# Moving the second layer's memory values ahead of the first layer's output projection

## The chip, the cores and the metric

The kernel runs on one core of a Trainium2 chip. The metric is the device time of one execution in microseconds. Three runs of the kernel before took 1002.79, 1003.25 and 1001.37 us, a median of 1002.79 us.

The engines are named as in the profile: PE is TensorE's matrix multiplication, PEld its loading of weights, DVE is VectorE, ACT is ScalarE, POOL is GpSimd, and SP is the engine whose queue issues all transfers. L120 is line 120 of the kernel.

## The reference

An encoder trunk of two layers works on 256 tokens of width 1024, in float32. Each layer computes:

```
h = x @ w_in                     # latents, differential q/k/v, memory queries, gates
o_mla, o_diff, o_mem = three attention branches
merged = sum of sigmoid(gate_i) * (o_i @ w_branch_i)
x = LayerNorm(alpha * x + merged @ w_out)
x = LayerNorm(alpha * x + relu(x @ w1)^2 @ w2)
```

The third branch is an attention into 256 memory tokens. Its keys and values are `mem @ mem_w_kv[l]`, split into two halves of 512 columns each. They depend on the memory and on the layer's weights alone, not on `x`, so those of the second layer can be computed at any time.

## The kernel before, in words

**Precision.** Every float32 operand is split into a high part, rounded by ACT, and a low part, the rest, computed by DVE. A product is made of three matmuls, high by high, high by low and low by high (`mm3`, L126 to L129). A weight block of 128 x 1024 values (512 KB) is loaded by SP into one of six `raw` buffers, and `wload` (L111) casts it on ACT (L120) and subtracts on DVE (L121) into one of eight `whl` buffers. A second ring, `whlx`, serves the held-back half of `w_out` and of the last `w2` blocks. `evac` (L151) brings a PSUM tile into SBUF in the same two parts, ACT first (L153), then DVE (L154).

**PSUM.** There are four `acc` tiles and four `sm` tiles, one bank each.

**Order.** The program is written as one long trace. A planner, which runs a model of the engines, then sets each engine's queue: what stands earlier in the trace goes first where it is ready by the model, and what stands later is pulled forward into free time. Each engine then works through its queue in order on the chip. In the attention part of a layer a list written by hand (`ORDER`) sets the order of the trace; its last steps in the first layer are those of branch E, whose results are transposed on PE (L714) and evacuated (L156 on ACT, L157 on DVE) into the operands of the output projection.

**Around the change.** After the last step of `ORDER` the first layer goes on in this order of the trace:

- the parameters of the first normalisation and the residual input `xn` are loaded;
- `load_memT` (L294) loads the transposed memory again and splits it;
- the output projection `wout` takes 96 matmuls in four accumulators: first blocks 0 to 3 for both halves of the tokens and both halves of the columns, then blocks 4 to 7 for the first 128 tokens, then for the others. In the profile these accumulators have the name `load_memT.acc`;
- the first 128 tokens are normalised and `fill_xT` (L195) transposes them in two groups of four on PE (L200) and evacuates each group (L153, L154) into a half of `xT`;
- `mem_keys` (L305) makes the second layer's memory keys, with four weight blocks;
- the other 128 tokens are normalised and filled into `xT`;
- `mem_values` (L320) makes the second layer's memory values: four weight blocks, two `sm` accumulators, 48 matmuls of 512 columns, and two evacuations;
- `mlp1(0)` (L942) begins. Its matmuls (`mm_wide`, L131) take the weights as the stationary operand and stream both parts of `xT` for all 256 tokens at once:

```
def both(k):
    PE.matmul(ps, lhsT=ws[k // 4][0][:, k % 4, sl], rhs=r2(k), start=k == 0, stop=k == KD - 1)
```

  so that the first of them needs the high and the low part of the first half of `xT` for the second 128 tokens too.

In the second layer there is no memory work. There the second fill of `xT` is followed at once by `MlpTokens.project(1)` (L554), which takes the `xT` of 128 tokens as the stationary operand by `mm3`: two matmuls with the high part, then one with the low part.

Of the kernel before, what the change touches and what calls it, by code (L numbers as in the profile page):

```python
# [21 lines left out]
DEPTH = 2  # L22
# [44 lines left out]
def encoder_trunk(ctx: ExitStack, tc: tile.TileContext, x, w_in, b_gate,  # L67
# [16 lines left out]
    def nm(s):  # L84
        uid[0] += 1
        return f"{stage[0]}.{s}_{uid[0]}"

    def acc_tile():
        return pp.tile([P, 512], F32, tag="acc", name=nm("acc"))
# [4 lines left out]
    def slot():  # L94
        return act.tile([P, 2, 512], F32R, tag="att", bufs=BUFS["att"], name=nm("att"))
# [15 lines left out]
    def wload(src, a, b, ring="whl", raw=None):  # L111
        if raw is None:
            raw = wraw(src, a, b)
        hl = wp.tile([P, 2, 1024], F32R, tag=ring, bufs=BUFS[ring], name=nm("whl"))
        hi, lo = (hl[:, s, :a * b].rearrange("p (a b) -> p a b", a=a) for s in range(2))
        split(hi, lo, raw)
        return hi, lo

    def split(hi, lo, src):
        S.copy(out=hi, in_=src)  # L120
        V.tensor_tensor(lo, src, f32v(hi), ALU.subtract)  # L121

    def wsrc(w2d, k0, nk, n0, nn):
        return w2d[k0 * P:(k0 + nk) * P, n0:n0 + nn].rearrange("(k p) n -> p k n", p=P)

    def mm3(ps, lh, ll, rh, rl, start, stop):  # L126
        PE.matmul(ps, lhsT=lh, rhs=rh, start=start, stop=False)  # L127
        PE.matmul(ps, lhsT=lh, rhs=rl, start=False, stop=False)  # L128
        PE.matmul(ps, lhsT=ll, rhs=rh, start=False, stop=stop)  # L129
# [21 lines left out]
    def evac(dst_h, dst_l, ps, scale=None):  # L151
        if scale is None:
            S.copy(out=dst_h, in_=ps)  # L153
            V.tensor_tensor(dst_l, ps, f32v(dst_h), ALU.subtract)  # L154
        else:
            S.activation(dst_h, ps, AF.Copy, scale=scale)  # L156
            V.scalar_tensor_tensor(dst_l, ps, scale, f32v(dst_h), ALU.mult, ALU.subtract)  # L157
# [37 lines left out]
    def fill_xT(xT, nat, t):  # L195
        for h in range(2):
            ps = sm_tile()
            for i in range(4):
                k = h * 4 + i
                PE.transpose(ps[:, i * P:(i + 1) * P], nat[:, k * P:(k + 1) * P], ident)  # L200
            pv = ps.rearrange("p (k q) -> p k q", k=4)
            ts = slice(t * P, (t + 1) * P)
            evac(xT[h][:, 0, :, ts], xT[h][:, 1, :, ts], pv)

    def xk(xT, k, t=None):
        v = xT[k // 4]
        ts = slice(0, T) if t is None else slice(t * P, (t + 1) * P)
        return v[:, 0, k % 4, ts], v[:, 1, k % 4, ts]
# [85 lines left out]
    def load_memT():  # L294
        stage[0] = "load_memT"
        mT = []
        for h in range(2):
            raw = wp.tile([P, 4, T], F32, tag="raw", bufs=BUFS["raw"], name=nm("memr"))
            nc.sync.dma_start(out=raw, in_=wsrc(mem_t, 4 * h, 4, 0, T))
            m = act.tile([P, 2, 4, T], F32R, tag="mT", bufs=2, name=nm("mT"))  # L300
            split(m[:, 0], m[:, 1], raw)
            mT.append(m)
        return mT
# [16 lines left out]
    def mem_values(l, mT, ptile):  # L320
        stage[0] = "mem_vals"
        pss = [ptile() for _ in range(2)]
        for c in range(4):
            wh, wl = wload(wsrc(w_mkv[l], 2 * c, 2, 512, 512), 2, 512)
            for i in range(2):
                k = 2 * c + i
                for t in range(2):
                    mh, ml = xk(mT, k, t)
                    mm3(pss[t], mh, ml, wh[:, i], wl[:, i], k == 0, k == KD - 1)
        Vt = []  # L330
        for t in range(2):
            v = slot()
            evac(v[:, 0, :], v[:, 1, :], pss[t])
            Vt.append(v)
        return Vt
# [269 lines left out]
    for l in range(DEPTH):  # L605
# [4 lines left out]
        if l == 0:  # L610
            K, Vt = [], []
# [292 lines left out]

        if l + 1 < DEPTH:
            memT = load_memT()
        pss = [acc_tile() for _ in range(4)]
        stage[0] = "wout"
        wo = {}
# [15 lines left out]
        for t in range(2):  # L925
# [9 lines left out]
                halfway = [m.project(0) for m in early]  # L935
            layernorm(xns[t], pss[2 * t:2 * t + 2], gb)
            fill_xT(xT, xns[t], t)
        if l + 1 < DEPTH:
            Vt = mem_values(l + 1, memT, sm_tile)


        def mlp1(j):  # L942
            stage[0] = "mlp1"
# [117 lines left out]
```

## Time and profile before

| | us |
|---|---|
| median of three runs | 1002.79 |
| the profiled execution's own time | 1001.16 |
| its span, first to last instruction | 999.4 |
| PE busy in the span | 985.4 (99%) |
| PEld busy | 851.3 (85%) |
| DVE busy | 753.4 (75%) |
| ACT busy | 588.8 (59%) |
| mean granted TensorE clock | 0.997 of full speed |

Matmuls overlap in the profile: one of 512 columns is listed with 0.39 us, and in a dense stretch the next starts 0.23 us after it. So the distance from one start to the next tells what a matmul costs, and the idle time listed for PE begins only where the listed end of the last one has passed. Transfers moved 181 MB, 181 GB/s over the span.

### The profile page before, as it was taken

Reading aid. Unit: us, or ns where it says so; the run is one execution under the profiler, and the core shown is the slowest. Engines: PE = TensorE matmul, PEld = TensorE weight load, DVE = VectorE, ACT = ScalarE, POOL = GpSimd, SP = SyncE. Lnnn points to the kernel's source line nnn. Section 1 sums busy time; section 2 is a strip of 40 time slices with the busy share of each in tenths; the row PEclk is TensorE's granted clock in tenths of the full one; section 3 lists DMA queues with packets and bytes.
Section 4 is the critical chain, followed back from the end, with each engine's and each line's share of the span. In section 5 each row is a group of like instructions: output and inputs, shape, how many; then the busy total and the mean of one; then the engine's idle time right before and its main releaser. Section 6 shows DMA issues by size and latency. Waiting matters only on the chain.

```text
span 999.4 us, 14511 instructions
## 1 busy us (share of the span) xinstructions
PE 985.4 (99%) x5315; PEld 851.3 (85%) x5315; DVE 753.4 (75%) x1164; ACT 588.8 (59%) x1060; POOL 45.6 (5%) x86
## 2 busy tenths in 40 slices
PE   9999999999999999999999999999999999999996
PEld 7888989888888888888889989898888878888885
DVE  6897889777897676656775988798688876666664
ACT  5975777766662554444624877778665525454540
POOL 0200001100000000000001110000000000000000
PEclk9999999999999999999999999999999999999998
DMA  9965455555794466665844755456457725766631
GB/s 302 319 209 146 121 148 169 171 156 159 243 308 123 151 192 196 195 192 175 292 130 154 228 151 148 129 158 186 130 157 261 232 76 177 228 186 191 188 127 43
DMA packets 103200, 181.06 MB, mean 181 GB/s; under 512 B 5965, under 2 KB 59481, under 8 KB 103129
## 3 DMA queue, kind: packets, MB, share of 16 engines
q1 hardware_dynamic: 103128, 180.14, 58.3%
q8 instruction: 42, 0.69, 0.3%
q14 instruction: 30, 0.24, 0.1%
HBM read 178.02 MB, written 2.10 MB: 180 GB/s over the span
## 4 chain that ended last, share of the span: by engine, by line
PE 94%; DVE 2%; ACT 2%; DMA 1%; issue 1%; POOL 0%; SPq 0%; DVEq 0%; ACTq 0%
PE mlp1.sm L135 11%; PE mlp1.sm L138 6%; PE mlp2.acc L127 6%; PE mlp2.acc L129 6%; PE mlp2.acc L128 6%; PE diff_proj.acc L127 5%; PE diff_proj.acc L128 5%; PE diff_proj.acc L129 5%; PE gate.acc L127 2%; PE gate.acc L128 2%; PE gate.acc L129 2%; PE branch.acc L127 2%; PE branch.acc L129 2%; PE branch.acc L128 2%; PE diff_att.sm L519 2%; PE mla_att.acc L128 1%
## 5 line engine op out<-in xcount | busy, mean ns | idle before, releaser
L121 DVE TENSOR_TENSOR mlp1.whl<-mlp1.raw,mlp1.whl 128x1024 fp32r<-128x1024 f32 x124 | 150.9, 1224 | 88.1 <-ACT mlp1.whl L120 85.4
L120 ACT CAST mlp1.whl<-mlp1.raw 128x1024 fp32r<-128x1024 f32 x124 | 129.9, 1052 | 88.7 <-PE mlp2.acc L129 41.7
L135 PE MATMUL mlp1.sm<-wout.xT,mlp1.whl 128*128 128x512 f32 x480 | 122.5, 392 | 0.0
L135 PEld LDWEIGHTS mlp1.sm<-wout.xT,mlp1.whl 128*128 128x128 f32 x480 | 86.3, 189 | 15.2
L127 PE MATMUL mlp2.acc<-mlp1.whl,mlp1.att 128*128 128x512 f32 x240 | 93.4, 389 | 0.0
L129 PE MATMUL mlp2.acc<-mlp1.whl,mlp1.att 128*128 128x512 f32 x240 | 93.4, 389 | 0.0
L128 PE MATMUL mlp2.acc<-mlp1.whl,mlp1.att 128*128 128x512 f32 x240 | 93.4, 389 | 0.0
L121 DVE TENSOR_TENSOR gate.whl<-gate.raw,gate.whl 128x1024 fp32r<-128x1024 f32 x48 | 58.4, 1219 | 18.0 <-ACT gate.whl L120 17.5
L138 PEld LDWEIGHTS mlp1.sm<-wout.xT,mlp1.whl 128*128 128x128 f32 x480 | 65.5, 190 | 4.7
L121 DVE TENSOR_TENSOR diff_proj.whl<-diff_proj.raw,diff_proj.whl 128x1024 fp32r<-128x1024 f32 x44 | 53.7, 1221 | 19.2 <-ACT diff_proj.whl L120 18.6
L138 PE MATMUL mlp1.sm<-wout.xT,mlp1.whl 128*128 128x256 f32 x480 | 66.9, 282 | 0.0
L120 ACT CAST gate.whl<-gate.raw 128x1024 fp32r<-128x1024 f32 x48 | 50.4, 1052 | 17.9 <-PE diff_proj.acc L129 5.8
L120 ACT CAST diff_proj.whl<-diff_proj.raw 128x1024 fp32r<-128x1024 f32 x44 | 46.5, 1056 | 21.2 <-PE diff_proj.acc L129 11.4
L537 ACT COPY mlp1.sum<-mlp1.sm 128x256 f32<-128x256 f32 x60 | 22.3, 372 | 54.8 <-PE mlp1.sm L135 54.8
L128 PEld LDWEIGHTS mlp2.acc<-mlp1.whl,mlp1.att 128*128 128x128 f32 x240 | 45.1, 188 | 9.4
L129 PEld LDWEIGHTS mlp2.acc<-mlp1.whl,mlp1.att 128*128 128x128 f32 x240 | 45.1, 188 | 9.4
L127 PEld LDWEIGHTS mlp2.acc<-mlp1.whl,mlp1.att 128*128 128x128 f32 x240 | 45.1, 188 | 9.4
L121 DVE TENSOR_TENSOR branch.whl<-branch.raw,branch.whl 128x1024 fp32r<-128x1024 f32 x32 | 39.1, 1221 | 14.7 <-ACT branch.whl L120 14.3
L120 ACT CAST branch.whl<-branch.raw 128x1024 fp32r<-128x1024 f32 x32 | 33.6, 1050 | 27.0 <-PE gate.acc L129 12.2
L127 PE MATMUL diff_proj.acc<-diff_proj.whl,mlp1.xT 128*128 128x512 f32 (+1 forms) x128 | 43.4, 340 | 0.2 <-ACT mlp1.xT L153 0.2
L128 PE MATMUL diff_proj.acc<-diff_proj.whl,mlp1.xT 128*128 128x512 f32 (+1 forms) x128 | 43.1, 338 | 0.0
L129 PE MATMUL diff_proj.acc<-diff_proj.whl,mlp1.xT 128*128 128x256 f32 (+1 forms) x128 | 42.9, 338 | 0.0
(472 smaller groups left out, 2533.9 us busy)
## 6 DMA issues: line engine op xcount, KB each, us to landing
mlp1.raw<-in_mlp_w_dram SPq DMA_DIRECT2D x124, 512.0 KB, 4.4
gate.raw<-in_w_in_dram SPq DMA_DIRECT2D x48, 512.0 KB, 3.7
branch.raw<-in_w_branch_dram SPq DMA_DIRECT2D x32, 512.0 KB, 3.8
diff_proj.raw<-in_w_dqk_dram SPq DMA_DIRECT2D x28, 512.0 KB, 4.2
diff_proj.raw<-in_w_in_dram SPq DMA_DIRECT2D x16, 512.0 KB, 3.8
wout.raw<-in_w_out_dram SPq DMA_DIRECT2D x16, 512.0 KB, 4.6
mq.raw<-in_w_in_dram SPq DMA_DIRECT2D x8, 512.0 KB, 4.7
mem_keys.raw<-in_mem_w_kv_dram SPq DMA_DIRECT2D x8, 512.0 KB, 5.6
```

What stands on the lines that cost most here:

```text
L120: S.copy(out=hi, in_=src)
L121: V.tensor_tensor(lo, src, f32v(hi), ALU.subtract)
L127: PE.matmul(ps, lhsT=lh, rhs=rh, start=start, stop=False)
L128: PE.matmul(ps, lhsT=lh, rhs=rl, start=False, stop=False)
L129: PE.matmul(ps, lhsT=ll, rhs=rh, start=False, stop=stop)
L135: PE.matmul(ps, lhsT=ws[k // 4][0][:, k % 4, sl], rhs=r2(k), start=k == 0, stop=k == KD - 1)
L138: PE.matmul(ps[:, 0, :], lhsT=ws[k // 4][1][:, k % 4, sl], rhs=r2(k)[:, 0, :], start=False, stop=False)
L519: PE.matmul(po[:, t * T:(t + 1) * T], lhsT=pT[:, hl, kt * T + t * P:kt * T + (t + 1) * P], rhs=vh[:, :, kt * T + j * P:kt * T + (j + 1) * ...
L537: S.copy(out=d, in_=ps[:, 1, :])
```

## The change

The call of `mem_values` for the second layer moves in the trace from behind the loop over the two token halves to the place right behind `load_memT`, ahead of the output projection. Nothing of what is computed changes, nor any size, buffer count or pool; `mem_values` still takes its two accumulators from the `sm` tiles. Its weight loads move ahead of those of `w_out` and of `mem_keys` in the trace.

```
         if l + 1 < DEPTH:
             memT = load_memT()
+            Vt = mem_values(l + 1, memT, sm_tile)
         pss = [acc_tile() for _ in range(4)]
         stage[0] = "wout"
...
             layernorm(xns[t], pss[2 * t:2 * t + 2], gb)
             fill_xT(xT, xns[t], t)
-        if l + 1 < DEPTH:
-            Vt = mem_values(l + 1, memT, sm_tile)
-
```

## Rows read from the trace of the kernel before

**Rows 1.** Page: busy us by engine; chain that ended last, share by engine.
```profile
PE 985.4 (99%) x5315; PEld 851.3 (85%) x5315; DVE 753.4 (75%) x1164; ACT 588.8 (59%) x1060; POOL 45.6 (5%) x86
...
PE 94%; DVE 2%; ACT 2%; DMA 1%; issue 1%; POOL 0%; SPq 0%; DVEq 0%; ACTq 0%
```

**Rows 2.** Waits of PE, whole span: waiter, releaser, total us, times, longest.
```profile
PE diff_proj.acc L274 <- ACT diff_proj.nat L763: 1.7, 1, 1.7
...
PE mlp1t.sm L571 <- DVE mlp1t.fr L544: 0.6, 1, 0.6
PE load_memT.acc L127 <- ACT branch.att L156: 0.5, 1, 0.5
...
PE mlp1t.sm L127 <- ACT wout.xT L153: 0.2, 1, 0.2
```

**Rows 3.** Timeline of PE, 296 to 306 us: start, us, instruction, [idle before, releaser].
```profile
296.26 1.04 PE L714 MATMUL branch.sm<-consts,branch.merged 128*128 128x128 f32 x8
297.84 0.50 PE L127 MATMUL load_memT.acc<-wout.whl,branch.att 128*128 128x512 f32 x1 [0.54 <-ACT branch.att L156]
...
299.77 0.60 PE L714 MATMUL branch.sm<-consts,branch.merged 128*128 128x128 f32 x4
300.30 0.50 PE L129 MATMUL load_memT.acc<-wout.whl,branch.att 128*128 128x512 f32 x1
...
304.97 0.60 PE L714 MATMUL branch.sm<-consts,branch.merged 128*128 128x128 f32 x4
305.32 0.48 PE L129 MATMUL load_memT.acc<-wout.whl,branch.att 128*128 128x512 f32 x1
```

**Rows 4.** Timeline of PE, 332 to 346 us.
```profile
332.91 1.04 PE L200 MATMUL layernorm.sm<-consts,branch.xn 128*128 128x128 f32 x8
333.70 0.47 PE L127 MATMUL mem_vals.sm<-mem_vals.whl,load_memT.mT 128*128 128x512 f32 x1
...
344.71 1.07 PE L135 MATMUL mlp1.sm<-wout.xT,mlp1.whl 128*128 128x512 f32 x4
```

**Rows 5.** Timeline of ACT and DVE, 333 to 337 us.
```profile
333.38 1.05 ACT L120 CAST mlp1.whl<-mlp1.raw 128x1024 fp32r<-128x1024 f32 x1
...
334.33 1.07 ACT L153 CAST wout.xT<-layernorm.sm 128x512 fp32r<-128x512 f32 x2
334.46 1.23 DVE L121 TENSOR_TENSOR mlp1.whl<-mlp1.raw,mlp1.whl 128x1024 fp32r<-128x1024 f32 x1
...
335.61 1.28 DVE L154 TENSOR_TENSOR wout.xT<-layernorm.sm,wout.xT 128x512 fp32r<-128x512 f32 x2
```

**Rows 6.** Timeline, second layer's fill of `xT` for the first tokens, 810 to 813 us.
```profile
810.99 1.03 PE L200 MATMUL layernorm.sm<-consts,branch.xn 128*128 128x128 f32 x8
...
811.63 1.07 ACT L153 CAST wout.xT<-layernorm.sm 128x512 fp32r<-128x512 f32 x2 [9.97 <-PE layernorm.sm L200]
812.24 0.69 DVE L154 TENSOR_TENSOR wout.xT<-layernorm.sm,wout.xT 128x512 fp32r<-128x512 f32 x1 [0.21 <-ACT wout.xT L153]
...
812.99 0.50 PE L129 MATMUL mlp1t.sm<-mlp1t.whl,wout.xT 128*128 128x512 f32 x1
```

**Rows 7.** Tile view of the memory values' accumulators: ns min/median/max, first and last start.
```profile
L128 PE MATMUL mem_vals.sm<-mem_vals.whl,load_memT.mT x16: 387/389/390, 334.0 to 344.3; 128*128 128x512 f32 x16
```

**Rows 8.** Timeline of ACT, 279 to 306 us: casts of weight blocks.
```profile
279.00 1.06 ACT L120 CAST wout.whl<-wout.raw 128x1024 fp32r<-128x1024 f32 x1 [1.79 <-PE branch.acc L129]
...
296.46 1.05 ACT L120 CAST mem_keys.whl<-mem_keys.raw 128x1024 fp32r<-128x1024 f32 x1 [0.31 <-PE branch.acc L129]
...
303.62 2.00 ACT L120 CAST mem_vals.whl<-mem_vals.raw 128x1024 fp32r<-128x1024 f32 x2 [1.36 <-PE load_memT.acc L129]
```

**Rows 9.** Windows: length, busy us by engine, granted clock, DMA share, GB/s.
```profile
46.00:49.00 3.00, 1.13 (x8) 0.89 (x9) 2.54 (x4) 3.00 (x6) 0.69 (x1) 1.00 0.98 321
...
250.00:297.00 47.00, 47.00 (x226) 39.43 (x225) 42.71 (x59) 30.37 (x44) 0.00 (x0) 1.00 0.82 273
```

**Rows 10.** Timeline of PE, the first 9 us of the span.
```profile
1.34 3.25 PE L340 MATMUL start.sm<-consts 128*128 128x128 f32 x14 [1.34 <-POOL consts masks.py:199]
4.57 1.22 PE L127 MATMUL diff_proj.acc<-start.whl,start.xT 128*128 128x512 f32 x2
...
8.61 0.62 PE L129 MATMUL diff_proj.acc<-diff_proj.whl,start.xT 128*128 128x512 f32 x2
```

More of the change, by code (lines that the diff above doesn't have):

```diff
@@ L906, in encoder_trunk @@
             memT = load_memT()
+            Vt = mem_values(l + 1, memT, sm_tile)
         pss = [acc_tile() for _ in range(4)]
@@ L937, in encoder_trunk @@
             fill_xT(xT, xns[t], t)
-        if l + 1 < DEPTH:
-            Vt = mem_values(l + 1, memT, sm_tile)
         def mlp1(j):
```

## The prediction

> **What bounds the kernel now.** I read the page first. PE is busy 985.4 of 999.4 us, and the chain of work that ended last runs over PE for 94% of the span [rows 1]. Busy time alone doesn't prove it, because matmuls overlap, so I read the waits of PE next. There are few, and the longest, 1.7 us, lies near 48 us, long before the change [rows 2]. Behind that the list has 0.5 us in front of the first layer's output projection, and in the second layer one of 0.6 us and some of 0.2. So PE is full, every matmul costs its distance to the next one, and a change of order can gain only what is left of those waits. It can lose whatever hole it opens. That makes two places worth reading start by start: where the memory values go to, and where they come from.
>
> **Where they go to.** In front of the projection PE transposes branch E's result and then needs its evacuation. A group of eight transposes starts at 296.26 and the next matmul at 297.84, 1.58 us later, with a listed idle of 0.54 [rows 3]. Where nothing is waited for, a group of eight is followed after 333.70 - 332.91 = 0.79 us [rows 4]. So 1.58 - 0.79 = 0.79 us are lost here (more than the listed idle, since the listed end of a matmul lies behind the time at which the next could start). A group of four is followed after 300.30 - 299.77 = 0.53 us where the low part is late, and after 305.32 - 304.97 = 0.35 us where it isn't [rows 3]: 0.18 us. Together 0.97 us. With the memory values ahead of the projection in the trace, 48 matmuls that need nothing of branch E stand ready for these two waits, and I count the whole 0.97 as gained. The ends are 0, if the planner still sends PE to transposes whose input is late on the chip, and 0.97.
>
> **Where they come from.** Today the second fill of xT is followed by the memory values, from 333.70 to 344.71, and these 11.0 us hide the evacuation of xT completely [rows 4]. With that cover gone, the next thing in the trace is mlp1, and its first matmul streams the high and low parts of xT for all tokens. It must wait for PE's transposes, then ACT's cast, then DVE's subtraction of the first half. I find nothing else for PE there: the memory keys stand ahead of the fill, and everything behind it needs xT. The chain in this very place: ACT first finishes a weight cast for mlp1, begun at 333.38, and starts the xT casts at 334.33. DVE works on the low part of that weight from 334.46 and starts on xT at 335.61 [rows 5]. One such subtraction takes 0.69 us and the matmul that waits for it starts 0.06 us after its end (812.24 + 0.69 = 812.93, then 812.99) [rows 6]. So mlp1 could start at 335.61 + 0.69 + 0.06 = 336.36, against 333.70 for the memory values: a hole of 2.66 us. The lower end is the same chain with ACT and DVE free, which the second layer shows: transposes at 810.99, the first use of the low part at 812.99, 2.00 us [rows 6] less the 0.79 that the transposes take anyway, 1.21 us. The upper end is one more weight block in DVE's queue ahead of xT, 1.23 us [rows 5]: 3.89 us. I take 2.66, because the weight cast that stands in the way is released by the memory keys, which keep their place right ahead of the fill; the planner then sees the same ready times there as now.
>
> **What else moves.** The 48 matmuls (three groups of 16 like that shown) cost PE the same anywhere [rows 7]: zero. Their four loads pass eight loads of the projection and four of the keys in SP's queue. In the 47 us ahead of the projection the transfers ran at 273 GB/s [rows 9], so four blocks of 0.524 MB put the projection's weights back by some 4 x 1.9 = 7.7 us. The first projection weight is cast at 279.00 now [rows 8], and would be at about 287; its matmuls, at 297.84 now, come 11 us later too. Without this cover the price would be the whole delay, but it would first have to use up some 18 us. The memory values' own weights take over the projection's place in the rings, so they are cast from about 279 on and needed at 297. Now they wait until the projection gives up its buffers, at 303.62 [rows 8]. The eight weight buffers stay as full as now: the memory values give theirs up first, then keys and mlp1 take them. The two sm tiles that the values hold leave two for branch E's transposes; should a group wait for one, the values' own matmuls are there to run. Their six steps on ACT and six on DVE hide under PE as they did: DVE and ACT were busy 42.7 and 30.4 of 47 us [rows 9]. All this I take at zero, with 0 to 0.8 us against it (one wait like that of rows 3).
>
> **The sum.** 2.66 - 0.97 = +1.69 us. On the profiled execution's own time that is 1001.16 + 1.69 = 1002.85 us. That execution (span 999.4 and 1.8 us around it) lies 1.63 us below the median of the runs, so the forecast for a median is 1002.79 + 1.69 = 1004.5 us: slower by 0.17%, just inside the 0.2% (2.0 us) which is about what a measurement of this kernel can tell from no change.
>
> **The rivals.**
> - *The evacuation comes first* (chance 0.2). The planner may put the casts of xT ahead of the weight cast; the hole is then 1.21 us, the sum +0.24, the time 1003.0. For it: xT stands earlier in the trace. Against it: so it does now, and the weight cast went first by 0.95 us [rows 5].
> - *A longer queue, and slower* (0.12). A second weight block of mlp1 comes free shortly before the fill, and DVE takes it too ahead of xT: 3.89 - 0.97 = +2.92, 1005.7 us. It decides from the point at which two buffers are given up within the last 2 us ahead of the transposes. For it: with the values gone, mlp1's loads run further ahead, so a raw block is always waiting. Against it: the other buffers then hold blocks that wait for xT themselves and can't be given up.
> - *The order doesn't change where it should* (0.08). If the values' weights aren't ready for PE at 297, the values run inside the projection or behind its first half; the wait of rows 3 stays and the hole opens all the same: +2.66, 1005.5 us. For it: the transfers are near their highest rate there. Against: 18 us of slack.
> - *The hole is filled* (0.05). Were a part of the memory keys kept back behind the transposes, nothing is lost and 0.97 gained: 1001.8 us. Against it: the keys' matmuls stand earlier in the trace and are ready.
> - *The clock falls in the hole* (0.05). TensorE's lower level is 1.2 GHz against 2.4. The start of the span shows the price: two matmuls take 1.22 us together at 4.57 and 0.62 at 8.61, and the slow stretch reaches from 1.34 to 8.61 at most [rows 10]; 7.3 us at half speed cost 3.6 us. Sum +5.3, 1008.1 us. Against it: an idle of 1.7 us near 48 us [rows 2] passed at a granted clock of 1.00 [rows 9]. The Trainium skill ("TensorE: Matmul & The Clock Gate", section "Why this matters for your kernels") warns that idle gaps between bursts of matmuls bring the clock down to half. That gap is the nearest that the trace has, and it did not; no row shows a hole of 2.7 us.
>
> **How the numbers follow.** The forecast has 0.5, the five rivals 0.5 together. Faster by over 0.2% would need 2.0 us, more than the 0.97 at the projection and about as much as that and the second layer's waits together, so it is left to measurement and to a luckier order in the second layer, which the planner makes anew: 0.06. Slower by over 0.2% (above 1004.8) takes nearly half of the forecast's own share, whose 1.69 is close to the bound, and the three dear rivals: 0.42. Within 0.2%: 0.52. The range runs from the filled hole to between the longer queue and the clock, 1001.6 to 1007.0 us. The forecast's own range, with 0.97 or little of it gained, is 1004.0 to 1005.5.
>
> **What would show it.** After the change PE has no wait at the first projection matmul, and the values run between branch E's transposes and the projection. The second fill is followed by an idle of PE whose releaser is DVE on xT (L154), 2.66 us from where the next matmul could have started. ACT shows a weight cast right ahead of the xT casts. I'd be wrong if no hole opens, if it is wider than 3.9 us, if the wait at the projection stays, or if the second layer's end moves by more than these two terms.

## The result, and the profile after

The changed kernel takes 1007.75 us (median of four runs, 1007.40 to 1008.33) against 1003.02 us for the kernel before on the same chip (four runs, 1001.37 to 1003.76): a ratio of 1.0051 [1.0039, 1.0063], 4.7 us slower. The forecast was +1.7 us and a range up to 1007.0.

The profiled execution took 1007.40 us with a span of 1005.6, against 1001.16 and 999.4. The busy time of PE is nearly that of [rows 1] (985.7 against 985.4 us), so the time went mostly into waiting:

```profile
PE 985.7 (98%) x5315; PEld 851.9 (85%) x5315; DVE 753.8 (75%) x1164; ACT 588.3 (59%) x1060; POOL 45.5 (5%) x86
...
PE 92%; DMA 3%; DVE 2%; ACT 1%; issue 1%; POOL 0%; SPq 0%; DVEq 0%; ACTq 0%
```

The waits of PE after the change, over the whole span (waiter, releaser, total us, times, longest). The accumulators of the projection, `load_memT.acc` in the rows of before, now have the name `mem_vals.acc`.

```profile
PE mem_vals.acc L127 <- DVE branch.merged L705: 2.8, 1, 2.8
...
PE mlp1.sm L135 <- DVE wout.xT L154: 2.4, 1, 2.4
```

The second line is new, and was forecast. The first is the wait of 0.5 us of [rows 2] that was to disappear: it has grown to 2.8. A wait in the first 11 us of the span has grown too (`diff_proj.acc` on `start.xT`, from 1.0 to 2.7 in total), but it costs nothing here: branch E's transposes start at 296.31 against 296.26 [rows 3]. The timeline of PE there, against [rows 3]:

```profile
296.31 1.04 PE L714 MATMUL branch.sm<-consts,branch.merged 128*128 128x128 f32 x8
300.18 0.53 PE L127 MATMUL mem_vals.acc<-wout.whl,branch.att 128*128 128x512 f32 x1 [2.83 <-DVE branch.merged L705]
...
302.58 1.91 PE L714 MATMUL branch.sm<-consts,branch.merged 128*128 128x128 f32 x8
304.14 0.78 PE L129 MATMUL mem_vals.acc<-wout.whl,branch.att 128*128 128x512 f32 x1
```

Behind branch E's transposes stands still the projection (`wout.whl`), not the memory values, and it starts 300.18 - 296.31 = 3.87 us after them, against 1.58 before: +2.29. Then eight transposes take 304.14 - 302.58 = 1.56 us where 0.79 was usual. The windows give the reason (length, busy us by engine, granted clock, DMA share, GB/s):

```profile
296.00:301.60 5.60, 2.77 (x17) 2.15 (x16) 5.60 (x8) 3.93 (x6) 0.00 (x0) 1.00 0.88 295
301.70:305.00 3.30, 3.30 (x13) 2.87 (x12) 2.82 (x7) 1.13 (x4) 0.00 (x0) 0.50 1.07 349
```

After the wait PE ran at a granted clock of 0.50, its level of 1.2 GHz, for about 3.4 us (worked out from the mean clocks of three stretches of 2 us from 300 to 306: 0.92, 0.50 and 0.73). The memory values came later, as their tile view shows (ns min/median/max, first and last start):

```profile
L127 PE MATMUL mem_vals.sm<-mem_vals.whl,load_memT.mT x16: 389/389/389, 309.2 to 319.4; 128*128 128x512 f32 x16
```

At the second fill of xT the forecast hole is there. PE, then ACT, then DVE, against [rows 4, 5]:

```profile
347.60 1.04 PE L200 MATMUL layernorm.sm<-consts,branch.xn 128*128 128x128 f32 x8
351.03 1.21 PE L135 MATMUL mlp1.sm<-wout.xT,mlp1.whl 128*128 128x512 f32 x4 [2.40 <-DVE wout.xT L154]
```

```profile
348.06 1.05 ACT L120 CAST mlp1.whl<-mlp1.raw 128x1024 fp32r<-128x1024 f32 x1
349.01 1.07 ACT L153 CAST wout.xT<-layernorm.sm 128x512 fp32r<-128x512 f32 x2
```

```profile
349.15 1.23 DVE L121 TENSOR_TENSOR mlp1.whl<-mlp1.raw,mlp1.whl 128x1024 fp32r<-128x1024 f32 x1
350.29 1.28 DVE L154 TENSOR_TENSOR wout.xT<-layernorm.sm,wout.xT 128x512 fp32r<-128x512 f32 x2
```

The weight of mlp1 is split ahead of xT on both engines. mlp1 follows the transposes after 351.03 - 347.60 = 3.43 us; less the 0.79 that they take, the hole costs 2.64 us.

From branch E's first transposes to mlp1's first matmul it was 344.71 - 296.26 = 48.45 us [rows 3, 4] and is 351.03 - 296.31 = 54.72: +6.27, which is the whole difference of the two spans (6.2). Of this 2.29 is the wait and 2.64 the hole. The remaining 1.34 is put down to the stretch at half clock, by subtraction, which takes all else as equal; the second wait of the prediction (0.18) is gone in the changed kernel, and with it the rest would be 1.52. An independent measurement of such a stretch stands with the last experiment. The medians differ by less (4.7) than the two profiled executions (6.2): that of before lay 1.86 us under its median.

So two questions: why did the wait grow, and what is the clock's part?

### The profile page after: what moved, and what is told of

The parts are those of the page before. It is cut to its first block, busy times and chain, and to the rows that moved or that the text cites. A ratio compares the mean times of both kernels' runs of the same rounds, so it can differ in the third digit from the quotient of the medians.

```text
span 1005.6 us, 14519 instructions
## 1 busy us (share of the span) xinstructions
PE 985.7 (98%) x5315; PEld 851.9 (85%) x5315; DVE 753.8 (75%) x1164; ACT 588.3 (59%) x1060; POOL 45.5 (5%) x86
## 4 chain that ended last, share of the span: by engine, by line
PE 92%; DMA 3%; DVE 2%; ACT 1%; issue 1%; POOL 0%; SPq 0%; DVEq 0%; ACTq 0%
PE mlp1.sm L135 11%; PE mlp1.sm L138 6%; PE mlp2.acc L127 6%; PE mlp2.acc L129 6%; PE mlp2.acc L128 6%; PE diff_proj.acc L127 4%; PE diff_proj.acc L128 4%; PE diff_proj.acc L129 4%; PE branch.acc L127 3%; PE branch.acc L129 3%; PE branch.acc L128 3%; PE gate.acc L127 2%; PE gate.acc L128 2%; PE gate.acc L129 2%; PE diff_att.sm L519 2%; PE mla_att.acc L128 1%
## 5 line engine op out<-in xcount | busy, mean ns | idle before, releaser
L127 PE MATMUL diff_proj.acc<-diff_proj.whl,start.xT 128*128 128x256 f32 (+1 forms) x126 | 41.8, 338 | 2.7 <-ACT start.xT L120 2.7
```

## The experiments

Times are medians, each beside the kernel before on the same chip. Experiments 1 to 4 ran on one chip, 5 to 8 on a second and 9 and 10 on a third, so what is compared across them is the ratio to the kernel before, and the distances inside the profiles. The changed kernel itself has its ratio of 1.0051 from the result and one of 1.0082 from experiment 10. "E to mlp1" is the distance used above, 48.45 us before and 54.72 in the changed kernel. A line of three dots in the code stands for lines left out.

**1. Other accumulators for the values.** The values' two accumulators come from the `acc` tiles.

```
-            Vt = mem_values(l + 1, memT, sm_tile)
+            Vt = mem_values(l + 1, memT, acc_tile)
```

> The changed kernel, but the memory values take their two accumulators from the acc tiles instead of the sm tiles. Theory A (the values could not fill the wait at branch E because branch E's four transposes hold all four sm tiles): now the values' matmuls run in that wait, PE's idle there falls from 2.8 us to under 0.3 and the clock stays at 1.00, while the hole at the second fill of xT stays at 2.4 us idle; in all +1.7 us over the kernel before (+0.2%), 4.6 us less than the changed kernel's profile. Rival B (the longer wait comes from more weight work in front of branch E, whatever tiles the values use): idle of 2 us or more stays there, +4 to +6 us. Rival C (the hole at xT is not caused by the missing cover): that idle changes too.

Measured: 1003.11 us against 1001.43, ratio 1.0018 [1.0006, 1.0030]; E to mlp1 49.98. The forecast was +1.69 us; measured is +1.68 [0.6, 3.0], and +1.53 by the distance in the profile. That the median fits to the hundredth is luck: six of its twelve runs lie at 1001.7 to 1002.7 us, the other six, all with a mean granted clock of 0.996 or less, at 1003.5 to 1006.0. PE:

```profile
296.11 1.04 PE L714 MATMUL branch.sm<-consts,branch.merged 128*128 128x128 f32 x8
296.91 0.48 PE L127 MATMUL mem_vals.acc<-mem_vals.whl,load_memT.mT 128*128 128x512 f32 x1
...
342.66 1.03 PE L200 MATMUL layernorm.sm<-consts,branch.xn 128*128 128x128 f32 x8
346.09 1.20 PE L135 MATMUL mlp1.sm<-wout.xT,mlp1.whl 128*128 128x512 f32 x4 [2.40 <-DVE wout.xT L154]
```

No wait; the values run right behind the transposes, and the hole at xT stays (346.09 - 342.66 = 3.43 us, as in the changed kernel). Yet DVE is as late with branch E as in the changed kernel:

```profile
302.13 0.68 DVE L705 TENSOR_TENSOR branch.merged<-branch.merged,consts 128x512 f32<-128x512 f32 x1
302.74 0.74 DVE L157 SCALAR_TENSOR_TENSOR branch.att<-branch.sm,branch.att 128x256 fp32r<-128x256 f32 x2
```

So lateness alone costs nothing as long as PE has work. The values were no such work in the changed kernel because of their tiles: branch E's transposes stand earlier in the trace and take the four `sm` tiles first, so the values' accumulators wait for the very evacuation that they were to hide.

**2. The projection's weights first in the trace.** Their eight blocks are loaded and split ahead of the values.

```
             memT = load_memT()
...
+            wo = {k: wload(wsrc(w_out[l], k, 1, 0, D), ...) for k in range(KD)}
             Vt = mem_values(l + 1, memT, sm_tile)
...
```

> The changed kernel, but the eight weight blocks of the output projection are loaded and split in the trace ahead of the memory values, as in the kernel before; the values keep their sm tiles. Theory D (the wait at branch E grew because the values' four blocks push the projection's weight splits back in the queues of ACT and DVE, ahead of branch E's merge and evacuation, where they wait for late transfers): the wait returns to about 0.5 us idle, no fall of the clock, the hole at xT stays at 2.4 us idle; in all about +2.6 us (0.26%). Rival A alone (only the sm tiles matter): the wait stays at about 2.8 us and the total at +5 to +6 us.

Measured: 1004.77 against 1001.43, ratio 1.0029 [1.0018, 1.0040]; E to mlp1 51.37. PE:

```profile
298.98 1.04 PE L714 MATMUL branch.sm<-consts,branch.merged 128*128 128x128 f32 x8
300.56 0.50 PE L127 MATMUL mem_vals.acc<-wout.whl,branch.att 128*128 128x512 f32 x1 [0.55 <-ACT branch.att L156]
```

The distance is 1.58 us again, as before; a second idle of 0.28 us stands behind the next transposes, and the hole stays. The growth of the wait thus comes from the weights' order; the 0.97 us are not gained, since the values still have no tiles. The forecast of +2.6 us lies within the interval (+3.34 [1.8, 4.0]). The profiled execution is the slowest of the twelve (1008.53 us): it has two stretches at half clock, near 51 us and behind the hole, and none at branch E.

**3. The values' weights alone in front,** in the kernel before; `value_weights` holds the four `wload` calls of `mem_values`, and the 48 matmuls stay in their old place.

```
             memT = load_memT()
+            vw = value_weights(l + 1)
...
-            Vt = mem_values(l + 1, memT, sm_tile)
+            Vt = mem_values(l + 1, memT, sm_tile, vw)
```

> The kernel before, with only the four weight blocks of the memory values loaded and split ahead of the output projection; their matmuls stay behind the second fill of xT. Theory D: the hole at xT is gone, the wait at branch E is as long as in the changed kernel (2.8 us idle, with or without the fall of the clock), in all +2.3 to +3.7 us. Rival (the place of the matmuls makes the wait, not the weights): no wait beyond 0.5 us, the time of the kernel before within 1 us.

Measured: 1005.05 against 1001.43, ratio 1.0038 [1.0025, 1.0051]; E to mlp1 51.60, no hole at xT. The wait is there without any matmul moved:

```profile
296.04 1.04 PE L718 MATMUL branch.sm<-consts,branch.merged 128*128 128x128 f32 x8
299.59 0.80 PE L127 MATMUL mem_vals.acc<-wout.whl,branch.att 128*128 128x512 f32 x1 [2.51 <-ACT branch.att L156]
```

The distance is 3.55 us, 1.97 more than before. A window from 299.3 to 302.5 us has a granted clock of 0.50 here too.

**4. Half of the keys behind the second fill,** in the changed kernel, to close the hole.

```
-                for _ in mem_keys(l + 1, memT, sm_tile, K):
-                    pass
+                keys = mem_keys(l + 1, memT, sm_tile, K)
+                next(keys)
...
             fill_xT(xT, xns[t], t)
+        if l + 1 < DEPTH:
+            for _ in keys:
+                pass
```

> The changed kernel, with the second half of the memory keys moved behind the second fill of xT. Theory (the hole at xT is only the missing cover): the 32 matmuls of the second half cover it, idle there under 0.2 us, the wait at branch E unchanged at 2.8 us with its fall of the clock; 2.4 to 2.7 us less than the changed kernel, +3.6 us over the kernel before. The first half alone must now cover the second normalisation, 5.5 us of matmuls against some 6.5 us, so up to 1 us may come back ahead of the transposes. Rival (the weight cast in front of the xT casts sets the time whatever PE does): a hole of 2 us stays somewhere between the fill and mlp1.

Measured: 1004.44 against 1001.43, ratio 1.0026 [1.0014, 1.0037]; E to mlp1 52.08. The hole is gone (the matmul behind the second fill's transposes starts 342.09 - 341.29 = 0.80 us after them), the wait at branch E stays (idle 3.0 us) and has a half-clock stretch behind it. The two costs are separate.

**5 and 6. Loads or splits?** In the changed kernel one value block is loaded once and split four times, or four are loaded and one is split.

```
+        one = wraw(wsrc(w_mkv[l], 0, 2, 512, 512), 2, 512) if l else None
...
-            wh, wl = wload(wsrc(w_mkv[l], 2 * c, 2, 512, 512), 2, 512)
+            wh, wl = wload(wsrc(w_mkv[l], 2 * c, 2, 512, 512), 2, 512, raw=one)
```

> The changed kernel with three of the memory values' four weight transfers left out: one block is loaded once and split four times, so the values are made of one block four times over and the second layer's memory branch is not the reference's. ACT and DVE have as many splits as before, SP and the transfers three blocks less ahead of the projection's. Theory D1 (late transfers of the projection's weights hold up the queues of DVE and ACT ahead of branch E): the idle at branch E falls from 2.8 us to at most 1.0, the hole at xT stays at 2.4, in all +2.6 to +3.5 us over the kernel before. Rival D2 (DVE has simply more splits to work through ahead of branch E): the idle stays at 2 us or more, +4 to +6 us.

Measured: 1007.86 against 1001.95, ratio 1.0061 [1.0045, 1.0078]; E to mlp1 53.97, idle at branch E 2.1, 0.3 and 0.7 us.

```
+        if l:
+            raws = [wraw(wsrc(w_mkv[l], 2 * c, 2, 512, 512), 2, 512) for c in range(4)]
+            first_w = wload(None, 2, 512, raw=raws[0])
...
-            wh, wl = wload(wsrc(w_mkv[l], 2 * c, 2, 512, 512), 2, 512)
+            wh, wl = first_w if l else wload(wsrc(w_mkv[l], 2 * c, 2, 512, 512), 2, 512)
```

> The changed kernel with all four transfers of the memory values' weights, but only the first block cast and split (of the others one column is copied), so the values are made of one block four times over. ACT and DVE have three splits less ahead of branch E (3.7 us of DVE), the transfers are as many. Theory D1 (late transfers): the idle at branch E stays near 2 to 3 us and the total at +4 to +6 us. Rival D2 (more splits on DVE): the idle falls to at most 1.0 us, +2.6 to +3.5 us. If both this and the kernel with one transfer shorten the wait by about half, both have a part in it.

Measured: 1006.93 against 1001.95, ratio 1.0049 [1.0034, 1.0063]; E to mlp1 53.40, idle 1.5 and 1.4 us. Both theories fell in their pure form: neither three loads nor three splits less takes the wait away. The trace of the second run suggests why. DVE there:

```profile
297.06 1.22 DVE L121 TENSOR_TENSOR mem_keys.whl<-mem_keys.raw,mem_keys.whl 128x1024 fp32r<-128x1024 f32 x1
...
298.80 2.35 DVE L121 TENSOR_TENSOR mem_keys.whl<-mem_keys.raw,mem_keys.whl 128x1024 fp32r<-128x1024 f32 x2
...
301.67 0.74 DVE L157 SCALAR_TENSOR_TENSOR branch.att<-branch.sm,branch.att 128x256 fp32r<-128x256 f32 x2
```

The planner filled the freed places with the keys' splits, and branch E stands behind these in DVE's queue. This would mean that it matters how many splits stand ahead of branch E's steps, not whose they are; that is read from the one trace and not tested by itself. In both runs the stretch at half clock lies behind the hole and not at branch E.

**7. The keys in front instead.** In the kernel before, the first half of the memory keys goes ahead of the projection, with accumulators from `acc`; the values stay behind the second fill.

```
             memT = load_memT()
+            K = []
+            keys = mem_keys(l + 1, memT, acc_tile, K)
+            next(keys)
...
-                K = []
-                for _ in mem_keys(l + 1, memT, sm_tile, K):
+                for _ in keys:
```

> The kernel before, with the first half of the memory keys (32 matmuls, two weight blocks) made ahead of the output projection, and the keys' tiles taken from the acc tiles; the values stay behind the second fill. If the wait at branch E is filled by the keys and nothing is opened elsewhere: idle there under 0.2 us, about 1.0 us less than the kernel before (0.999), too little to be told from no change. Rival: the first half is missing as cover of the second normalisation, or the second half waits for an acc tile of the projection: a new wait of 1 to 3 us in front of the second transposes, 1.000 to 1.002.

Measured: 1000.20 against 1001.95, ratio 0.9985 [0.9976, 0.9993]: a little faster than the kernel before, which the changed one was not. E to mlp1 is 47.43 us, 1.02 less than before, where the forecast had put 0.97 on the waits at branch E; the difference of the medians (1.75 [0.7, 2.4]) is larger, and no trace shows the rest. The waits are filled:

```profile
296.33 0.60 PE L714 MATMUL branch.sm<-consts,branch.merged 128*128 128x128 f32 x4
296.69 1.17 PE L135 MATMUL mem_keys.acc<-load_memT.mT,mem_keys.whl 128*128 128x512 f32 x4
```

**8. Work in the hole.** Experiment 1 with 20 unused transposes behind the second fill, to keep PE busy there.

```
             fill_xT(xT, xns[t], t)
+        if l + 1 < DEPTH:
...
+            spare = sm_tile()
+            for _ in range(20):
+                PE.transpose(spare[:, :P], xns[1][:, :P], ident)
```

> The version with the values in acc tiles, with twenty transposes of 128 columns into a spare sm tile added behind the second fill of xT, whose results nobody uses: PE is busy in the hole for 20 x 0.11 = 2.2 us, and mlp1 starts when it did. Theory (part of the hole's price is a fall of the clock that some runs have and others not): the same span as the best runs of the version with acc tiles (about 1000 to 1001 us), but its runs with a lower granted clock become as rare as those of the kernel before; the median falls by 0.5 to 1.2 us to about +0.6 to +1.3 us over the kernel before. Rival (the hole's price is its length alone): the median and the spread of the granted clock stay as they were, +1.8 us.

Measured: 1002.83 against 1001.95, ratio 1.0011 [1.0002, 1.0020]; E to mlp1 49.99 as in experiment 1. The idle ahead of mlp1 falls from 2.40 to 0.22 us. The time fits the theory (+0.6 to +1.3 us), but +0.88 [0.2, 2.0] can't be told from the +1.68 [0.6, 3.0] of experiment 1. The mean granted clock is 0.996 or less in 5 of its 12 runs, against 6 of 12 in experiment 1, and the theory wanted this to become as rare as in the kernel before (2 of 23 runs). So the hole is at most one cause of such runs, and how many it makes can't be told from this.

**9. The late splits behind branch E.** In the changed kernel the loads and splits of the projection's second four blocks are issued behind branch E's last evacuation (the two instructions of `evac` on ACT and DVE).

```
-                wo[k] = wload(wsrc(w_out[l], k, 1, 0, D), ...)
+                if l == 0 and k >= KD - HOLD_OUT:
+                    with tc.issue_after(last_evac[0]), tc.issue_after(last_evac[1]):
+                        wo[k] = wload(wsrc(w_out[l], k, 1, 0, D), 1, D, ring="whlx")
...
```

> The changed kernel with the second four of the projection's weight blocks (their loads and their splits on ScalarE and VectorE) issued behind the last evacuation of branch E; nothing else. Theory D (weight splits that come late stand ahead of branch E's merge and evacuation in the in-order queues of ScalarE and VectorE): TensorE's idle time at branch E's transposes falls from 2.8 us to 0.8 us or less, no stretch at half clock follows it, the hole of 2.4 us at the second fill of xT stays, and the time is 2 to 3.5 us over the kernel before. Rival (the wait comes from branch E's own work, or from the allocation of the tiles alone): idle of 2 us or more stays there, and the time is 4 to 5 us over.

Measured: 1004.18 against 1001.13, ratio 1.0031 [1.0017, 1.0045]; E to mlp1 50.39. PE:

```profile
296.13 1.48 PE L715 MATMUL branch.sm<-consts,branch.merged 128*128 128x128 f32 x12
297.75 0.50 PE L127 MATMUL mem_vals.acc<-wout.whl,branch.att 128*128 128x512 f32 x1 [0.15 <-ACT branch.att L156]
...
346.52 1.19 PE L135 MATMUL mlp1.sm<-wout.xT,mlp1.whl 128*128 128x512 f32 x4 [2.39 <-DVE wout.xT L154]
```

The wait falls from 2.83 to 0.15 us of idle, no half clock follows it, and the hole stays, as the theory of the queues said. Of the 3.05 us [1.7, 4.5] this part of the kernel explains 1.94 in the profile (span 1001.4); the rest is within the interval. The evacuation is early again (first L157 at 298.92, against 302.96 in the changed kernel):

```profile
297.79 1.22 DVE L121 TENSOR_TENSOR wout.whl<-wout.raw,wout.whl 128x1024 fp32r<-128x1024 f32 x1
298.92 0.75 DVE L157 SCALAR_TENSOR_TENSOR branch.att<-branch.sm,branch.att 128x256 fp32r<-128x256 f32 x2
```

**10. The changed kernel again,** beside the run above.

> The changed kernel again, beside the run above on the same chip. Every theory: 4 to 5.5 us over the kernel before, a wait of 2 to 3 us at branch E's transposes and a hole of 2.4 us at the second fill of xT. The clock's part is what may differ: if the stretch of 3.41 us at half clock is in every execution, the time is 1007 to 1008 us and its spread is small; if it is in some, executions near 1006 us are among them.

Measured: 1009.92 us (1008.14 to 1010.49) against 1001.13, ratio 1.0082 [1.0066, 1.0097]. More than expected (1007 to 1008 us). Its profiled execution, the slowest of the four (1010.49 us), has three stretches at half clock, not one. The three are the second, fourth and sixth line of these windows; each stands behind a line in which PE waited:

```profile
46.00:49.00 3.00, 1.19 (x9) 0.96 (x10) 2.54 (x4) 3.00 (x6) 0.63 (x1) 1.00 0.99 309
49.40:52.70 3.30, 3.30 (x13) 2.93 (x12) 3.24 (x5) 2.37 (x5) 0.00 (x0) 0.50 1.02 381
297.00:301.80 4.80, 1.80 (x13) 1.35 (x11) 4.80 (x7) 4.39 (x7) 0.00 (x0) 1.00 0.88 307
302.00:305.20 3.20, 3.20 (x8) 2.55 (x9) 3.20 (x5) 0.27 (x2) 0.00 (x0) 0.50 1.08 355
350.00:353.00 3.00, 0.60 (x5) 0.35 (x3) 2.88 (x5) 2.19 (x4) 0.00 (x0) 1.00 0.50 160
353.20:356.40 3.20, 3.20 (x13) 2.87 (x12) 0.56 (x1) 0.00 (x0) 0.00 (x0) 0.50 0.58 172
```

The last of them gives the price. From mlp1's first matmul to the second layer's first one it is 528.87 - 351.03 = 177.84 us in the first profile of this kernel, without a stretch, and 531.99 - 352.62 = 179.37 here, with one. PE in the first profile (mlp1's first matmul is shown above), then in this one:

```profile
528.87 0.50 PE L127 MATMUL diff_proj.acc<-diff_proj.whl,mlp1.xT 128*128 128x512 f32 x1 [0.24 <-ACT mlp1.xT L153]
```

```profile
352.62 0.83 PE L135 MATMUL mlp1.sm<-wout.xT,mlp1.whl 128*128 128x512 f32 x2 [2.40 <-DVE wout.xT L154]
...
531.99 0.50 PE L127 MATMUL diff_proj.acc<-diff_proj.whl,mlp1.xT 128*128 128x512 f32 x1 [0.24 <-ACT mlp1.xT L153]
```

So a stretch costs 1.53 us. The other profiles agree: the same distance is 179.26 to 179.38 us in the three others that have a stretch there (experiments 2, 5 and 6) and 177.71 to 177.84 in all that have none. Two stretches more than in the first profile make 3.06, and the two spans differ by 1008.7 - 1005.6 = 3.1.

## Why the prediction was wrong, point by point

**The hole at xT: right.** Forecast 2.66 us, measured 2.64, by the forecast chain (a weight of mlp1 ahead of xT on ACT and DVE). The rivals "the evacuation comes first" and "a longer queue" are out. The rival "the hole is filled" took a rearranged kernel (experiment 4).

**The gain of 0.97 us: wrong in this kernel, right in size.** The failed step is the sentence that "48 matmuls that need nothing of branch E stand ready for these two waits". They do need something of it: their `sm` tiles. The prediction saw the four tiles but had it the wrong way round ("The two sm tiles that the values hold leave two for branch E's transposes"): branch E, earlier in the trace, is served first. Experiment 1 gives them other tiles: the wait is filled, and what is left is near the forecast (+1.53 us in the profile); experiment 7 fills the same waits with the keys and gains 1.02.

**What else moves, "at zero, with 0 to 0.8 us against it": wrong, and the larger error.** The transfers came late about as worked out: the projection's first cast moved from 279.00 [rows 8] to 288.39, 9.4 us where 7.7 was the estimate. ACT before, and then after:

```profile
280.85 6.02 ACT L120 CAST wout.whl<-wout.raw 128x1024 fp32r<-128x1024 f32 x6 [0.80 <-DMA wout.raw<-in_w_out_dram]
...
297.41 0.64 ACT L156 ACTIVATE branch.att<-branch.sm 128x256 fp32r<-128x256 f32 x2
```

```profile
283.36 1.06 ACT L120 CAST mem_vals.whl<-mem_vals.raw 128x1024 fp32r<-128x1024 f32 x1 [1.89 <-PE gate.acc L129]
285.63 1.05 ACT L120 CAST mem_vals.whl<-mem_vals.raw 128x1024 fp32r<-128x1024 f32 x1 [1.21 <-PE branch.acc L129]
288.39 1.06 ACT L120 CAST wout.whl<-wout.raw 128x1024 fp32r<-128x1024 f32 x1 [1.71 <-PE gate.acc L129]
...
297.86 1.99 ACT L120 CAST wout.whl<-wout.raw 128x1024 fp32r<-128x1024 f32 x2 [0.47 <-DMA wout.raw<-in_w_out_dram]
299.75 0.65 ACT L156 ACTIVATE branch.att<-branch.sm 128x256 fp32r<-128x256 f32 x2
```

The slack of 18 us was measured to the matmuls that use these weights. But on ACT, shown above, and on DVE

```profile
298.35 1.22 DVE L121 TENSOR_TENSOR wout.whl<-wout.raw,wout.whl 128x1024 fp32r<-128x1024 f32 x1
299.49 0.68 DVE L705 TENSOR_TENSOR branch.merged<-branch.merged,consts 128x512 f32<-128x512 f32 x1
300.09 2.35 DVE L121 TENSOR_TENSOR wout.whl<-wout.raw,wout.whl 128x1024 fp32r<-128x1024 f32 x2
302.36 0.68 DVE L705 TENSOR_TENSOR branch.merged<-branch.merged,consts 128x512 f32<-128x512 f32 x1
302.96 1.62 DVE L157 SCALAR_TENSOR_TENSOR branch.att<-branch.sm,branch.att 128x256 fp32r<-128x256 f32 x4
```

the late splits stand in queues that are worked off in order, ahead of branch E's merge (L705) and evacuation (L156, L157). These had no slack at all. The first projection matmul needs ACT's part alone: L156 began 2.34 us later than before (299.75 against 297.41) and the matmul 2.34 us later (300.18 against 297.84), so what set the wait was ACT's queue; the merge on DVE that the list of waits names ended at nearly the same time. Experiment 3 shows this part alone, experiments 2 and 9 take it away. Its price is 2.29 us of waiting, where a gain of 0.79 had been entered.

What made the projection's weights later on the chip than the planner's order supposes isn't settled: experiments 5 and 6 didn't separate loads from splits. The rows above show one thing that the prediction passed over. It let the values' weights "take over the projection's place in the rings", but only half of the projection's blocks lie in `whl`; the other half has `whlx`, and before, six of them were cast in one go from 280.85. The values' four all need `whl`, and two of their casts and the projection's first waited 1.89, 1.21 and 1.71 us for matmuls of the gates and branches, that is, most likely, for a `whl` buffer to come free; the next waited for transfers. No experiment tests this by itself.

**The clock.** It got a chance of 0.05 and the hole as its place. In the first profile it fell behind the wait at branch E, and in others (experiment 10) behind the hole and near 48 us too. The section "Why this matters for your kernels" of the Trainium skill ("TensorE: Matmul & The Clock Gate") says that idle gaps between bursts of matmuls bring the clock down to half. The trace agrees in kind, but the gaps behind which it fell here (listed idle of 1.71, 2.40 and 2.83 us) are shorter than those that the section warns of. The argument against it, one idle of 1.7 us that passed, was too thin, and the window shown for it couldn't bear it: it ends at 49 us [rows 9], and in experiment 10 the same window is at 1.00 as well, with the half clock behind it. The price was overstated: 3.6 us, against 1.53 measured.

**The sum as it should have been.** 2.29 for the wait and 2.64 for the hole make 4.93 us, and each stretch at half clock adds 1.3 to 1.5. The number of stretches differs from execution to execution (one and three in the two profiles of this kernel); that this is also the difference between its two medians, +4.7 and +8.8 us, is likely but not shown, as only profiled executions have a trace. As a whole the forecast missed by 3.0 us of +4.7, and its own signs said so: the wait at the projection stayed. The rival nearest to what happened was "the order doesn't change where it should" (+2.66): right that the wait would stay, but not that it would grow.

## What to carry to other kernels

Moving independent work forward fills a wait only if that work holds every resource it needs, tiles included, without the step it is to hide; look up who takes the ring of tiles first. A load that is put back is measured against the next thing in the queue of the engine that prepares it, not against the matmul that uses the data. Fill a wait with the part of the work that nothing else needs as a cover (here half of the keys, on tiles that branch E doesn't use: 0.9985 [0.9976, 0.9993]), and leave the part that covers another wait where it is.

## What the runs showed of the hardware

In a kernel whose PE is 98% busy, single waits of 1.7 to 3.1 us of idle were followed in some executions by about 3.4 us at a granted clock of 0.50, and such a stretch cost about 1.5 us on top of the wait. It isn't certain. Over the twelve profiles of this document, the half clock came behind the wait of 1.71 us near 48 us in 2 of 12 and behind the hole of 2.40 us at xT in 4 of 7. Behind the wait at branch E it came in all 4 in which the idle was 2.5 to 3.1 us (the changed kernel twice, experiments 3 and 4), and in neither of the two in which the longest was 2.1 and 1.5 us (experiments 5 and 6).
